# Key and query scratch with the rows of a map side by side: key loads with 64 outer rows in place of four

## The chip, the cores and the metric

One core of one Trainium2 chip runs the whole program. The metric is the device time of one execution in microseconds (us). TensorE (PE), VectorE (DVE), ScalarE (ACT), GpSimd (POOL) and SyncE (SP) each take their instructions in order; transfers run on 16 DMA engines and are issued by SP or ACT.

## The reference

One inference step of a backbone of two layers. 1024 latent tokens and 128 context tokens go through the same weights. Each layer has three groups of heads: differential attention (four heads of 64, two softmax maps per head), a bidirectional gated DeltaNet and a bidirectional mLSTM (four heads each, in chunks), then an output projection and a SwiGLU. The attention, cut to what matters here:

```python
def diff_attention(q, k, v, lam):            # q, k: (B, tokens, 4 heads, 2 maps, 64)
    ...
        s = jnp.einsum('bqhmd,bkhmd->bhmqk', qi, k).astype(jnp.float32) * scale
        p = jax.nn.softmax(s, axis=-1)
        w = p[:, :, 0] - lam * p[:, :, 1]
        return jnp.einsum('bhqk,bkhe->bqhe', w.astype(v.dtype), v)
...
    k_all = jnp.concatenate([axial_rope(ak), k_ctx.astype(ak.dtype)], axis=1)
    a_out = diff_attention(axial_rope(aq), k_all, v_all, diff_lambda(lqk, lam_init))
```

Latent queries attend to 1024 latent and 128 cached keys, context queries to the 128 context keys.

## The kernel before

Latent and context tokens stand in one row of NT = 1152 columns, in three groups of 384 (`GW`). A layer is a sequence of stages: the projections and the preparation of the three mixers (`w_in`), the attention beside the scan of the DeltaNet and the mLSTM (`mixers`), the output projection and the feed-forward part. No order is written out by hand: each engine's instructions are put in order by a scheduler at build time, which plans the whole program with costs of its own. It also gives every transfer one of a few completion semaphores, so that an issue can have to wait until an earlier transfer with the same one has landed.

Products are made in pieces of fp32r: a value is split into a high part (an ACT copy) and a rest (a DVE subtraction). Queries and keys go through DRAM scratch in that form. `blk_a` projects a block, applies the rotary embedding to its two parts p (the even and the odd elements of a head's 64), and `put` splits each of them into `kh` (two buffers of 128 rows, high and rest) and stores it: `put_k` into KD with one transfer, 128 outer rows on both sides, `put_q` into QD with two, one for high and one for rest, whose DRAM side has four outer rows (one for each pair of head and map). Both are issued by SP.

In the attention stage a head loads two tiles K, one per map m, and V, then goes through its queries in blocks of 256 (the last has the 128 context queries). A K tile has 128 partitions: 32 rows of p = 0 and 32 of p = 1 in the high part, then the same of the rest, each row 1280 keys long. It is one transfer whose DRAM side, `(l p)`, has four outer rows of 32 inner ones. A Q tile holds the high queries in both halves of the partitions, so that a product with K adds both parts of the key, and the rest of the queries beside it; each half is one transfer with 64 outer rows and, inside, m and l. All of these loads are issued by ACT, between its own copies and exponentials. There are three buffers for K, so that the first map's K of the next head can be loaded early, while the second has to wait until the head before has used its first.

```python
for hl in range(2):
    nc.tensor.matmul(p[:, :w], lhsT=q[:, m, hl, 128 * j:128 * j + 128],
                     rhs=K[m][:, 128 * ks[0]:128 * ks[0] + w], start=hl == 0, stop=hl == 1)
nc.vector.tensor_scalar(out=e[:, GW * i:GW * i + w], in0=p[:, :w], scalar1=0.125, ..., accum_out=mx[:, i:i + 1])
```

These are the scores s (L1250) and the DVE pass over them (L1251); ACT's exponential follows (L1256), the difference of the maps, the transposes t and the output o.

Beside the attention run the last inverses of the DeltaNet's chunks (`prep2`: matmuls into px, L879 to L909, each waiting for small copies, T and X on ACT, qs and qq on DVE) and then the scan (matmuls into z and y), whose operands SP loads from scratch (rd, rm, vr, v, qk, cq; L1062 loads qk).

Of the kernel before, what the change touches and what calls it, by code (L numbers as in the profile page):

```python
# [9 lines left out]
F32 = mybir.dt.float32  # L10
# [7 lines left out]
P = 128  # L18
# [4 lines left out]
NT = NL + NC  # L23
# [47 lines left out]
class Kern:  # L71
# [362 lines left out]
    def open_s(self, l):  # L434

        S = self.S = {}
        dt = lambda n, shape: self.dr.tile(shape, F32, name=f"{n}{l}")
        S["BT"] = dt("BT", [P, 6, CVO])
        S["CQK"] = dt("CQK", [P, 4, NT])
        S["V1"] = dt("V1", [NCH, P, H, 65])  # L440
        S["BC"] = dt("BC", [NCH, P, 512])
        S["QD"] = dt("QD", [8, 2, 64, NT])
        S["KD"] = dt("KD", [2, 2, 2, P, NT + P])
        S["VD"] = dt("VD", [10, P, 512])
        S["ND"] = dt("ND", [2, NCH, P, H, P])
        S["RD"] = dt("RD", [2, NCH, P, 1024])
        S["GR"] = dt("GR", [2, 16, NT])
        S["VK"] = dt("VK", [NCH, P, 768])
        S["RM"] = dt("RM", [2, NCH, P, 768])
        S["CAT"] = dt("CAT", [KB, P, NT])  # L450
        ed, pe = ExitStack(), ExitStack()
        self.dn = ed.enter_context(self.pool("psdn", PSUM))
        self.pp = pe.enter_context(self.pool("pspp", PSUM))
        return ed, pe
# [472 lines left out]
    def put(self, dst, src, w):  # L927

        t = self.t(self.pr, [P, 2, GW], "kh", 2, F32R)[:, :, :w]
        self.nc.scalar.copy(t[:, 0], src)  # L930
        self.nc.vector.tensor_sub(t[:, 1], src, t[:, 0].bitcast(F32))
        if len(dst) == 1:
            self.nc.sync.dma_start(dst[0], t.bitcast(F32))
        else:
            for i in range(2):
                self.nc.sync.dma_start(dst[i], t[:, i].bitcast(F32))

    def put_k(self, hf, p, cols, src, w):
        self.put([self.S["KD"][hf, :, p, :, cols].rearrange("l r t -> r l t")], src, w)

    def put_q(self, hf, p, cols, src, w):
        self.put([self.S["QD"][4 * hf:4 * hf + 4, hl, 32 * p:32 * p + 32, cols] for hl in range(2)], src, w)

    def blk_a(self, l, qk, hf, u):

# [265 lines left out]
    def attention(self, l):  # L1211

        nc, S, at, pa = self.nc, self.S, self.at, self.pa
# [9 lines left out]
        for h in range(H):  # L1223
            K = []
            for m in range(2):
                k = self.t(at, [P, NT + P], "K", 3, F32R)
                r = 64 * (h % 2) + 32 * m
                nc.scalar.dma_start(k.bitcast(F32), S["KD"][h // 2].rearrange("l p r t -> (l p) r t")[:, r:r + 32, :])
                K.append(k)
            V = self.t(at, [P, 10, 128], "V", 2)  # L1230
            nc.scalar.dma_start(V, S["VD"][:, :, 128 * h:128 * h + 128].rearrange("s p e -> p s e"))
            for q0 in range(0, NT, 256):
                nq = min(256, NT - q0)
                q = self.t(at, [P, 2, 2, 256], "Q", 3, F32R)
                for hh in range(2):
                    nc.scalar.dma_start(q[64 * hh:64 * hh + 64, :, :, :nq].bitcast(F32), S["QD"][2 * h:2 * h + 2, :, :, q0:q0 + nq].rearrange("m l p t -> p m l t"))
                ctx = q0 >= NL
                kt = [9] if ctx else list(range(9))
                groups = [kt] if ctx else [kt[0:3], kt[3:6], kt[6:9]]
# [1 line left out]
                for j in range(nq // 128):  # L1241
                    es, zs = [], []
                    for m in range(2):
                        e = self.t(at, [P, NT], "e", 4)
                        mx = self.t(at, [P, 4], "mx", 4)
                        for i, ks in enumerate(groups):
                            w = 128 * len(ks)
                            p = self.ps(pa, "s", 2)
# [24 lines left out]
                    for i, ks in enumerate(groups):  # L1273
                        n = len(ks)
                        p = self.ps(pa, "t", 1)
# [278 lines left out]
```

## Time and profile before

| What | before |
|---|---|
| median of 3 runs | 3789.91 us (3785.78 to 3790.86) |
| profiled execution, its time | 3786.69 us |
| its span | 3784.9 us |
| PE busy | 3537.8 us (93%) |
| DVE busy | 2294.3 us (61%) |
| ACT busy | 1135.1 us (30%) |
| POOL busy | 655.4 us (17%) |
| DMA moved | 434.12 MB, mean 115 GB/s |

The span is the time from the first to the last instruction of the profiled execution. Busy times leave out the issue of transfers. PEclk is the clock that was granted to PE, as a share of the full one. "q" behind an engine's name is its queue, where transfers are issued; in a chain of waits a transfer's piece is the time for which the chain rested on it.

### The profile page before, as it was taken

What the parts mean: (1) busy time and instruction counts of PE and PEld (TensorE: products, weight loads), DVE (VectorE), ACT (ScalarE), POOL (GpSimd) and SP (SyncE); (2) the same over time, 40 slices, a digit from 0 to 9 for tenths busy, and PEclk for the clock granted to TensorE, in tenths of its full rate; (3) what the DMA queues carried; (4) which work ended last, traced back from release to release, by engine and by line L of the source; (5) the groups of instructions that cost most, each with busy time, mean ns of one, the idle gap of its engine ahead of it and who ended that gap; (6) DMA issues with size and microseconds to landing.
All of it is one profiled execution on the core that took longest, in us unless ns stands there. A gap on an engine that the chain in (4) does not pass through costs nothing.

```text
span 3784.9 us, 59404 instructions
## 1 busy us (share of the span) xinstructions
PE 3537.8 (93%) x22770; PEld 3372.2 (89%) x22770; DVE 2294.3 (61%) x5361; ACT 1135.1 (30%) x2383; POOL 655.4 (17%) x903
## 2 busy tenths in 40 slices
PE   7999979988999999999999998889889999999998
PEld 6997777887899999999989877778778999999997
DVE  7896677778455566654475568377775434333435
ACT  5323316445241111111243431244553311111111
POOL 2014231455020000000020234025631000000001
PEclk8999988999899999999999999889899999999999
DMA  5376624864212222221132663467442111111111
GB/s 208 134 249 232 221 80 122 235 201 144 84 59 84 78 84 83 91 78 48 59 110 96 220 230 102 130 162 227 132 142 67 34 39 46 46 38 40 51 45 56
DMA packets 277090, 434.12 MB, mean 115 GB/s; under 512 B 24648, under 2 KB 186504, under 8 KB 276552
## 3 DMA queue, kind: packets, MB, share of 16 engines
q1 hardware_dynamic: 213336, 289.68, 23.7%
q10 hardware_dynamic: 63472, 140.66, 12.3%
q8 instruction: 180, 2.95, 0.3%
q14 instruction: 102, 0.84, 0.1%
HBM read 315.85 MB, written 114.39 MB: 114 GB/s over the span
## 4 chain that ended last, share of the span: by engine, by line
PE 75%; DMA 10%; DVE 9%; issue 3%; ACT 1%; POOL 1%; SPq 0%; ACTq 0%; POOLq 0%; DVEq 0%
PE pd L189 6%; PE pd L190 6%; PE pd L191 6%; PE pg L191 5%; PE pu L190 5%; PE pu L191 5%; PE pu L189 5%; PE pg L190 5%; PE pg L189 5%; PE dn L189 4%; PE dn L190 4%; PE dn L191 4%; DMA K<-KD 3%; PE s L1250 3%; PE o L1284 2%
## 5 line engine op out<-in xcount | busy, mean ns | idle before, releaser
L362 DVE SCALAR_TENSOR_TENSOR x<-pd,mod,x 128x256 f32<-128x256 f32 (+1 forms) x832 | 405.0, 514 | 598.6 <-PE pd L191 597.4
L183 ACT CAST wh<-wr 128x1024 fp32r<-128x1024 f32 (+1 forms) x219 | 229.1, 1047 | 873.8 <-PE pu L190 462.1
L184 DVE TENSOR_TENSOR wl<-wr,wh 128x1024 fp32r<-128x1024 f32 (+1 forms) x219 | 268.7, 1233 | 167.6 <-ACT wh L183 167.1
L189 PE MATMUL pd<-hh,wh 128*128 128x384 f32 x1056 | 359.3, 340 | 7.3 <-DVE x L362 5.1
L189 PE MATMUL pg<-uh,wh 128*128 128x384 f32 x1056 | 357.2, 338 | 2.6 <-ACT uh L342 2.6
L190 PE MATMUL pg<-ul,wh 128*128 128x384 f32 x1056 | 357.9, 339 | 1.2 <-DVE ul L347 1.2
L299 POOL TENSOR_TENSOR nacc<-nacc,nsq 128x384 f32<-128x384 f32 x48 | 52.2, 1087 | 1770.7 <-issue 1572.5
L189 PE MATMUL pu<-uh,wh 128*128 128x384 f32 x1056 | 355.8, 337 | 0.0
L190 PE MATMUL pu<-ul,wh 128*128 128x384 f32 x1056 | 355.8, 337 | 0.0
L190 PE MATMUL pd<-hl,wh 128*128 128x384 f32 x1056 | 355.5, 337 | 0.0
L191 PE MATMUL pg<-uh,wl 128*128 128x384 f32 x1056 | 354.7, 339 | 0.0
L191 PE MATMUL pd<-hh,wl 128*128 128x384 f32 x1056 | 354.2, 337 | 0.0
L191 PE MATMUL pu<-uh,wl 128*128 128x384 f32 x1056 | 350.7, 337 | 0.0
L189 PE MATMUL dn<-uh,wh 128*128 128x384 f32 x864 | 299.4, 347 | 5.7 <-ACT gw L956 4.4
L190 PE MATMUL dn<-ul,wh 128*128 128x384 f32 x864 | 298.3, 345 | 0.0
L191 PE MATMUL dn<-uh,wl 128*128 128x384 f32 x864 | 297.8, 345 | 0.1
L1250 PE MATMUL s<-K,Q 128*128 128x384 f32 (+1 forms) x800 | 222.9, 389 | 61.2 <-DMA K<-KD 23.5
L1251 DVE TENSOR_SCALAR_CACHE_REDUCE e<-s 128x384 f32<-128x384 f32 (+1 forms) x400 | 208.8, 540 | 76.4 <-PE s L1250 72.3
L189 PEld LDWEIGHTS pd<-hh,wh 128*128 128x128 f32 x1056 | 198.7, 188 | 18.6 <-issue 7.7
L189 PE MATMUL dn<-wh,uh 128*128 128x256 f32 (+1 forms) x624 | 184.6, 296 | 24.1 <-DVE gw L558 19.7
L1250 PEld LDWEIGHTS s<-K,Q 128*128 128x128 f32 x800 | 136.4, 205 | 78.4 <-DVE e L1251 33.5
L189 PEld LDWEIGHTS pg<-uh,wh 128*128 128x128 f32 x1056 | 199.5, 189 | 4.5 <-ACT uh L342 2.8
(354 smaller groups left out, 8224.4 us busy)
## 6 DMA issues: line engine op xcount, KB each, us to landing
wr<-in_w_gu_dram ACTq DMA_DIRECT2D x88, 512.0 KB
aw<-in_w_mod_dram SPq DMA_DIRECT2D x96, 256.0 KB
wr<-in_w_dn_dram ACTq DMA_DIRECT2D x44, 512.0 KB
wr<-in_w_st_dram ACTq DMA_DIRECT2D x36, 512.0 KB
rd<-RD SPq DMA_DIRECT2D x36, 512.0 KB
aw<-in_w_mod_dram SPq DMA_DIRECT2D x32, 512.0 KB
Q<-QD ACTq DMA_DIRECT2D x64, 256.0 KB
RM<-em SPq DMA_DIRECT2D x36, 384.0 KB
```

The costliest lines, as they stand in the source:

```text
L183: nc.scalar.copy(hi, r)
L184: (eng or nc.vector).tensor_tensor(out=lo, in0=r, in1=hi.bitcast(F32), op=ALU.subtract)
L189: mm(out, lhsT=wh, rhs=xh, start=start, stop=False)
L190: mm(out, lhsT=wh, rhs=xl, start=False, stop=False)
L191: mm(out, lhsT=wl, rhs=xh, start=False, stop=stop)
L299: (nc.gpsimd if k in PST else nc.vector).tensor_tensor(out=self.acc[g], in0=self.acc[g], in1=s, op=ALU.add)
L362: nc.vector.scalar_tensor_tensor(out=x[g][k][:, lo:hi], in0=ps[:, lo:hi], scalar=gate[:, k, cnd:cnd + 1], in1=x[g][k][:, lo:hi], op0=ALU.m ...
L1250: nc.tensor.matmul(p[:, :w], lhsT=q[:, m, hl, 128 * j:128 * j + 128], rhs=K[m][:, 128 * ks[0]:128 * ks[0] + w], start=hl == 0, stop=hl == 1)
L1251: nc.vector.tensor_scalar(out=e[:, GW * i:GW * i + w], in0=p[:, :w], scalar1=0.125, scalar2=None, op0=ALU.mult, op1=ALU.max, accum_out=mx[ ...
L1284: nc.tensor.matmul(po, lhsT=WT[i][:, a], rhs=V[:, kx, :], start=kx == kt[0], stop=kx == kt[-1])
```

## The change

Both scratches get another order of their axes, in which the row r of a map and its part p are neighbours: a map's 64 rows, (r p), lie side by side. The K load then has 64 outer rows per transfer, one transfer for the high half of the partitions and one for the rest; the Q load has one transfer for each half and each of high and rest, four in place of two; `put` stores queries as it stores keys, with one transfer of 128 outer rows. The number of bytes is the same everywhere.

```diff
--- before.py
+++ after.py
@@ -439,8 +439,8 @@
         S["CQK"] = dt("CQK", [P, 4, NT])
         S["V1"] = dt("V1", [NCH, P, H, 65])
         S["BC"] = dt("BC", [NCH, P, 512])
-        S["QD"] = dt("QD", [8, 2, 64, NT])
-        S["KD"] = dt("KD", [2, 2, 2, P, NT + P])
+        S["QD"] = dt("QD", [2, 2, P, 2, NT])
+        S["KD"] = dt("KD", [2, 2, P, 2, NT + P])
         S["VD"] = dt("VD", [10, P, 512])
         S["ND"] = dt("ND", [2, NCH, P, H, P])
         S["RD"] = dt("RD", [2, NCH, P, 1024])
@@ -929,17 +929,13 @@
         t = self.t(self.pr, [P, 2, GW], "kh", 2, F32R)[:, :, :w]
         self.nc.scalar.copy(t[:, 0], src)
         self.nc.vector.tensor_sub(t[:, 1], src, t[:, 0].bitcast(F32))
-        if len(dst) == 1:
-            self.nc.sync.dma_start(dst[0], t.bitcast(F32))
-        else:
-            for i in range(2):
-                self.nc.sync.dma_start(dst[i], t[:, i].bitcast(F32))
+        self.nc.sync.dma_start(dst.rearrange("l r t -> r l t"), t.bitcast(F32))
 
     def put_k(self, hf, p, cols, src, w):
-        self.put([self.S["KD"][hf, :, p, :, cols].rearrange("l r t -> r l t")], src, w)
+        self.put(self.S["KD"][hf, :, :, p, cols], src, w)
 
     def put_q(self, hf, p, cols, src, w):
-        self.put([self.S["QD"][4 * hf:4 * hf + 4, hl, 32 * p:32 * p + 32, cols] for hl in range(2)], src, w)
+        self.put(self.S["QD"][hf, :, :, p, cols], src, w)
 
     def blk_a(self, l, qk, hf, u):
 
@@ -1225,15 +1221,19 @@
             for m in range(2):
                 k = self.t(at, [P, NT + P], "K", 3, F32R)
                 r = 64 * (h % 2) + 32 * m
-                nc.scalar.dma_start(k.bitcast(F32), S["KD"][h // 2].rearrange("l p r t -> (l p) r t")[:, r:r + 32, :])
+                for lk in range(2):
+                    nc.scalar.dma_start(k[64 * lk:64 * lk + 64].bitcast(F32), S["KD"][h // 2, lk, r:r + 32].rearrange("r p t -> (r p) t"))
                 K.append(k)
             V = self.t(at, [P, 10, 128], "V", 2)
             nc.scalar.dma_start(V, S["VD"][:, :, 128 * h:128 * h + 128].rearrange("s p e -> p s e"))
+            r0 = 64 * (h % 2)
             for q0 in range(0, NT, 256):
                 nq = min(256, NT - q0)
                 q = self.t(at, [P, 2, 2, 256], "Q", 3, F32R)
                 for hh in range(2):
-                    nc.scalar.dma_start(q[64 * hh:64 * hh + 64, :, :, :nq].bitcast(F32), S["QD"][2 * h:2 * h + 2, :, :, q0:q0 + nq].rearrange("m l p t -> p m l t"))
+                    for hl in range(2):
+                        nc.scalar.dma_start(q[64 * hh:64 * hh + 64, :, hl, :nq].bitcast(F32),
+                                     S["QD"][h // 2, hl, r0:r0 + 64, :, q0:q0 + nq].rearrange("(m r) p t -> (r p) m t", m=2))
                 ctx = q0 >= NL
                 kt = [9] if ctx else list(range(9))
                 groups = [kt] if ctx else [kt[0:3], kt[3:6], kt[6:9]]
```

In the changed kernel the K load stands at L1225, the Q load at L1235, V at L1228 and `put` at L932.

**ACT's queue at the start of attention in layer 0, before:** the loads of the first head (KD_122, QD_121 and VD_123 are the scratches) between copies of T and X for the inverses.

```order
L1228 DMA K_7842<-KD_122 128x1x1280
L861 COPY X_676_3285<-Nd_2455 32x4x32 x4
L1228 DMA K_7844<-KD_122 128x1x1280
L1231 DMA V_7846<-VD_123 128x10x128
L1236 DMA Q_7848<-QD_121 64x4x256 x2
L864 COPY T_680_3289<-cv_3297 32x4x32 x2
L864 COPY T_681_3290<-cv_3363 32x4x32 x2
L1236 DMA Q_8016<-QD_121 64x4x256 x2
L1236 DMA Q_8184<-QD_121 64x4x256
```

The same place in the changed kernel:

```order
L1225 DMA K_7830<-KD_122 64x1280
L861 COPY X_676_3285<-Nd_2455 32x4x32 x4
L1225 DMA K_7830<-KD_122 64x1280
L1225 DMA K_7833<-KD_122 64x1280 x2
L864 COPY T_680_3289<-cv_3297 32x4x32 x2
L1228 DMA V_7836<-VD_123 128x10x128
L861 COPY X_678_3287<-Nd_2456 32x4x32 x4
L864 COPY T_681_3290<-cv_3363 32x4x32 x2
L1235 DMA Q_7838<-QD_121 64x2x256 x4
L1235 DMA Q_8008<-QD_121 64x2x256
L864 COPY T_680_3289<-cv_3297 32x4x32 x2
```

The two K loads are four, Q's loads for a block are four, and both copies of T that stood behind Q's first block now stand ahead of it.

**PE at the same place, before:** the last px matmuls ahead of the first scores.

```order
L893 MATMUL px_3783<-Nd_2455,qs_744_3774 32x32 x4
L893 MATMUL px_3789<-Nd_2456,qs_746_3781 32x32 x4
L901 MATMUL px_3795<-T_680_3289,w_733_3715 64x64 x4
L901 MATMUL px_3802<-T_681_3290,w_734_3723 64x64 x4
L1250 MATMUL s_7854<-K_7842,Q_7848 128x384 x2
L1250 MATMUL s_7858<-K_7842,Q_7848 128x384 x2
L909 MATMUL px_3809<-X_676_3285,qq_3800 64x64 x4
```

In the changed kernel, from the same px matmul (px_3795) on:

```order
L901 MATMUL px_3795<-T_680_3289,w_733_3715 64x64 x4
L901 MATMUL px_3802<-T_681_3290,w_734_3723 64x64 x4
L909 MATMUL px_3809<-X_676_3285,qq_3800 64x64 x4
L909 MATMUL px_3816<-X_678_3287,qq_3807 64x64 x4
L879 MATMUL px_3839<-cv_3297,w_755_3823 32x32 x4
L879 MATMUL px_3846<-cv_3363,w_756_3831 32x32 x4
L887 MATMUL px_3853<-qs_758_3844,Nd_2455 32x32 x4
L887 MATMUL px_3859<-qs_760_3851,Nd_2456 32x32 x4
L893 MATMUL px_3865<-Nd_2455,qs_758_3844 32x32 x4
L1250 MATMUL s_7846<-K_7830,Q_7838 128x384
L1250 MATMUL s_7850<-K_7830,Q_7838 128x384
L1250 MATMUL s_7846<-K_7830,Q_7838 128x384
```

Seven more rows of px, 28 matmuls, now stand ahead of the first scores.

**SP in the preparation of layer 0, where the queries are stored, before** (kh is the split block, CQK, GR and VK are scratches of the mLSTM, rope the rotary table):

```order
L936 DMA QD_121<-kh_4793 4x32x384 x2
L936 DMA QD_121<-kh_4798 4x32x384 x2
L961 DMA rope_4933<-in_rope_dram 128x2x256
L936 DMA QD_121<-kh_4869 4x32x384
L936 DMA QD_121<-kh_4874 4x32x384
L756 DMA c_487_2464<-CQK_118 128x4x128
L790 DMA gr_2495<-GR_126 2x8x128
L790 DMA gr_2524<-GR_126 2x8x128
L936 DMA QD_121<-kh_4869 4x32x384
L936 DMA QD_121<-kh_4874 4x32x384
```

In the changed kernel:

```order
L932 DMA QD_121<-kh_4793 128x2x384
L932 DMA QD_121<-kh_4797 128x2x384
L957 DMA rope_4929<-in_rope_dram 128x2x256
L756 DMA c_487_2464<-CQK_118 128x4x128
L790 DMA gr_2495<-GR_126 2x8x128
L790 DMA gr_2524<-GR_126 2x8x128
L932 DMA QD_121<-kh_4867 128x2x384
L932 DMA QD_121<-kh_4871 128x2x384
L768 DMA VK_127<-vk_2471 128x768
```

Two transfers for a kh have become one, and the mLSTM's loads stand ahead of the second pair.

## Rows read from the trace of the kernel before

**Rows 1.** The chain that ended last, shares of the span by line.

```profile
PE pd L189 6%; PE pd L190 6%; PE pd L191 6%; PE pg L191 5%; PE pu L190 5%; PE pu L191 5%; PE pu L189 5%; PE pg L190 5%; PE pg L189 5%; PE dn L189 4%; PE dn L190 4%; PE dn L191 4%; DMA K<-KD 3%; PE s L1250 3%; PE o L1284 2%
```

**Rows 2.** Engines in the attention stages: stretch, length, busy time of each, PEclk, DMA, GB/s.

```profile
545.00:945.00 400.00, 340.50 (x3013) 310.81 (x3011) 306.75 (x1023) 200.20 (x486) 165.76 (x211) 0.90 0.61 175
...
2415.00:2815.00 400.00, 338.52 (x2709) 311.38 (x2708) 293.04 (x980) 188.92 (x447) 166.43 (x207) 0.88 0.61 175
```

**Rows 3.** The chain that ended last, in order of time: start, length, what.

```profile
549.15 24.47 DMA Q<-QD
574.59 1.62 PE s L1250 x4
...
2421.59 14.11 DMA K<-KD
2435.71 16.06 DMA Q<-QD
2451.91 1.62 PE s L1250 x4
...
2739.64 12.88 DMA K<-KD
```

**Rows 4.** Engines in eleven load stretches of the attention stages, and their sum.

```profile
549.00:574.00 25.00, 10.37 (x163) 9.32 (x160) 6.89 (x22) 2.20 (x8) 0.00 (x0) 0.53 0.65 157
653.00:667.20 14.20, 10.93 (x137) 9.62 (x133) 10.72 (x39) 6.86 (x19) 2.63 (x3) 0.98 0.65 157
...
2421.50:2452.00 30.50, 15.59 (x262) 13.90 (x255) 10.80 (x34) 3.14 (x11) 0.00 (x0) 0.55 0.66 167
...
sum 183.10, PE 117.74 PEld 108.05 DVE 111.16 ACT 60.83 POOL 64.23; mean PE 10.70 PEld 9.82 DVE 10.11 ACT 5.53 POOL 5.84
```

**Rows 5.** Engines in five stretches of these stages without such a load, sum.

```profile
sum 296.00, PE 281.82 PEld 267.29 DVE 247.69 ACT 154.14 POOL 151.72; mean PE 56.36 PEld 53.46 DVE 49.54 ACT 30.83 POOL 30.34
```

**Rows 6.** Engines in two short stretches: Q alone moves, K alone moves.

```profile
635.50:637.50 2.00, 2.00 (x17) 1.93 (x17) 1.91 (x9) 1.31 (x2) 0.00 (x0) 1.00 0.92 230
671.00:675.00 4.00, 4.00 (x38) 3.18 (x37) 2.31 (x11) 1.14 (x5) 0.55 (x1) 0.70 0.24 99
```

**Rows 7.** DMA issues: queue, count, size of one.

```profile
Q<-QD ACTq DMA_DIRECT2D x64, 256.0 KB
...
K<-KD ACTq DMA_DIRECT2D x16, 640.0 KB
```

**Rows 8.** Timeline of ACT and its queue at both starts; [idle before <-releaser].

```profile
546.31 1.12 ACTq L1228 DMA_DIRECT2D K<-KD  x1
...
549.15 16.90 ACTq L1236 DMA_DIRECT2D Q<-QD  x2
566.15 0.30 ACT L864 COPY T<-cv 32x128 f32<-32x128 f32 x1 [17.45 <-issue]
...
2450.56 0.62 ACT L864 COPY T<-cv 32x128 f32<-32x128 f32 x2 [24.14 <-DMA Q<-QD]
```

**Rows 9.** Waits of SP's queue: total us, times, longest.

```profile
SPq L1062 <- DMA K<-KD: 20.4, 2, 10.2
```

**Rows 10.** The chain again: a write of KD and the longest of QD.

```profile
277.70 4.75 DMA KD<-kh
...
302.04 10.61 DMA QD<-kh
```

**Rows 11.** Engines while the chain rested on a QD write.

```profile
299.00:316.00 17.00, 11.52 (x40) 8.25 (x40) 9.60 (x21) 4.18 (x9) 3.47 (x5) 0.67 0.57 184
```

**Rows 12.** Issues by line: count, duration in ns min/median/max, first and last start.

```profile
L1228 ACTq DMA_DIRECT2D K<-KD x16: 537/558/1124, 546.3 to 2739.6; - x16
...
L1236 ACTq DMA_DIRECT2D Q<-QD x80: 581/590/16234, 549.1 to 2776.8; - x80
...
L182 ACTq DMA_DIRECT2D wr<-in_w_gu_dram x88: 334/334/335, 1006.3 to 3681.4; - x88
...
L1149 SPq DMA_DIRECT2D cq<-CQK x32: 359/371/662, 692.7 to 2697.8; - x32
```


## Prediction

> **What bounds the kernel now.** I read the chain of work that ended last first, then cut its one suspicious item into stretches. TensorE (PE) carries three quarters of the chain, but one transfer, the load of K from the scratch KD, holds 3% of it [rows 1], that is 0.03 × 3784.9 = 113 us, the largest share of any transfer. All of it lies in the two attention stages, one per layer, each 400 us long, in which PE is busy 340.50 and 338.52 us and DVE 306.75 and 293.04 [rows 2]: 60 us of PE are idle in each. In order of time the reader should see the chain come to rest on a load at every head: at a stage's start on the first Q (24.47 us in layer 0; K 14.11 and then Q 16.06 in layer 1) with the first score matmul right behind, and later on K again, the shortest time 12.88 us [rows 3]. There are seven K pieces, four Q pieces and one V piece of that kind.
>
> I then asked for engine time in eleven stretches, one for each load that the chain rests on in these stages (in two places two neighbouring ones together). They last 183.1 us and PE works 117.74 of them: 65.4 us idle, more than half of the 121 us idle in both stages. The two starts alone leave 25.0 − 10.37 = 14.6 and 30.5 − 15.59 = 14.9 idle; the stretch at 653 us leaves only 3.3 of 14.2 [rows 4], since px work (the inverses of the DeltaNet chunks) stands in PE's order ahead of the waiting scores. In five stretches of the same stages without such a load and near full clock PE works 281.82 of 296 us, 95.2% [rows 5]. So the loads are what is left to win, and PE's cover is what limits the win.
>
> Why the loads are slow shows in a stretch in which K moves alone: a DMA share of 0.24, that is four of 16 engines, and 99 GB/s. Where Q moves alone, from 64 outer rows, the share is 0.92 and the rate 230 GB/s [rows 6]. K is 640 KB a map, Q 256 KB a half [rows 7]. A Q queued behind K ends only when its share on the four busy engines ends.
>
> The slow K does harm beyond PE. ACT issues these loads in order with its copies: one pair of Q issues held its queue for 16.90 us, and the copy of T behind it, which px waits for, started after 17.45 us of idling; in layer 1 a copy of T waited 24.14 us for Q [rows 8]. SP, which feeds the scan, lost 20.4 us at one of its loads to K [rows 9].
>
> **The change, part by part.** The sum is made against the profiled execution, 3786.69 us (span 3784.9); the median of the three runs is 3.2 us above it.
>
> *A, the starts of the two stages.* From the first K issue to the first score: 574.59 − 546.31 = 28.3 us [rows 3, 8] and 2451.91 − 2421.59 = 30.3 us [rows 3]. In the new order the same bytes stand ahead of the first score: K twice and V, 3 × 655,360 B (V has K's size: 10 × 128 rows of 128 floats), and Q, 2 × 262,144 B [rows 7]: 2.49 MB. At the 230 GB/s of the 64-row Q loads that takes 10.8 us; the first issue (1.12 us in layer 0, rows 8), the last landing and SP's transfers for px, which run beside it on the same engines, come on top, and I take 14.5. The waits shrink by 13.8 and 15.8. The new PE order has 28 more px matmuls ahead of the first score, and the T copies that they need now stand ahead of Q in ACT's order, so px fills the shorter wait and is not itself held up; I charge 2.6 for it. **A = −27**, bounds −15 (half is eaten by px, which runs from copy to copy) and −40 (px hides all of it and the clock comes back sooner: the 10.37 + 15.59 us of PE work in these stretches ran at a granted clock of 0.53 and 0.55, near the lower of its two levels, 1.2 GHz [rows 4]; at 2.4 it would be some 13 us less).
>
> The Trainium skill speaks against loading in halves: "DMA: Bandwidth & Descriptors" (Rules for kernel authors) says that transfers to two partition halves serialize and one of 128 partitions should be used, and "SBUF — State Buffer" (Door 1: The DMA port swizzle) gives 196 GB/s for 64 partitions against 328 for 128 at 1 MiB. The Q row, with loads of both halves in flight, shows 230, between the two. By 196 the 10.8 us would be 12.7, by 328 they would be 7.6: the halves may leave some 3 us a start unused, and do not turn the sign.
>
> *B, the later loads.* The nine other stretches hold 183.1 − 55.5 = 127.6 us with 117.74 − 25.96 = 91.8 us of PE work [rows 4]: 35.8 idle. K alone falls from 12.88 us or more to 655,360 B / 230 GB/s = 2.8 plus some 2 for issue and landing. That saving, 8 or more, exceeds the idle of most stretches, and the Q, V and SP loads behind K are freed too. At the clean share [rows 5] 91.8 us of work take 96.4: −31.2 at best. Behind a vanished wait comes the next one, DVE's pass over the scores or ACT's exponential, so I take two thirds: **B = −22**, bounds −8 (a shorter wait only hands over to the next) and −31.2.
>
> *C, the writes of QD.* 48 writes with 4 outer rows become 24 with 128. The chain rests on QD writes four times, the longest 10.61 us; a KD write, which has 128 outer rows already, stands there with 4.75 [rows 10]. What waits is ACT's next conversion (two kh buffers), and behind it work of the mLSTM that PE needs. But PE is mostly covered: around the longest it worked 11.52 of 17 us [rows 11]. KD's own writes keep shape and number. **C = −6**, bounds 0 and −15.
>
> *D, more issues on ACT.* 16 K issues at a median 558 ns become 32 with one outer dimension, as wr has (334): +1.8 us. 80 Q issues at 590 ns become 160 with two, as cq has (371 on SP): +12.2 [rows 12]. ACT is busy 200.20 and 188.92 of 400 us [rows 2], and its cover is its idling before exponentials; if that were gone, all 14.0 would count. **D = +3**, bounds 0 and +14. On SP 24 issues fall away, off the path: 0.
>
> Sum: −27 − 22 − 6 + 3 = −52. 3786.7 − 52 = 3734.7 for a profiled run; 3789.9 − 52 = **3738 us** for the median. At the bounds: −15 − 8 + 14 = −9 and −40 − 31.2 − 15 = −86.
>
> **The rivals.**
> *The waits change hands* (0.18). The new order of all engines differs throughout, since the scheduler planned it afresh; PE and DVE stand near each other in the stages [rows 2], so a shorter load wait may be taken over by DVE, or by ACT between them. For it: the stretch at 653 us, where PE idles 3.3 of 14.2 [rows 4]. Against it: the starts, where ACT works 2.20 of 25 us and PE 10.37 [rows 4]. Time: A and B at their low bounds, C nothing, D +5: −18, 3772 us.
>
> *The whole chain gives* (0.13). Every load wait goes, the clock stays up, SP's loads arrive early: A and B at their high bounds, C −15, and D nothing: −86, 3704 us. For it: copies of T and SP's loads stood behind K [rows 8, 9]. Against it: PE cannot be busier than all the time, and most stretches have little idle.
>
> *ACT's queue becomes the bound* (0.06), the slower case. Each Q and K issue may have to wait for the landing of an earlier transfer that shares its semaphore, and ACT's copies and exponentials wait behind it, as once in layer 0 for 17.45 us [rows 8]. With twice as many issues back to back at each of the six later head changes such a stop can recur there. It decides from 52 / 6 = 8.7 us a change on; at 12 us it costs 72 and the time is 3790 + 20 = 3810 us. Against it: what has to land does so in about a third of the time.
>
> *The change doesn't spread the loads* (0.03). If 64 outer rows stayed on four engines, only D would be left, +3 to +14: about 3797 us. The Q row, 64 outer rows at a share of 0.92, speaks against it [rows 6]. The Trainium skill ("DMA: Bandwidth & Descriptors", Why a DMA increments its semaphore by 16 and not by 1) says that the engines are the largest number up to 16 that divides the outer counts of both sides: 4 for 4 and 128, 16 for 64 and 64; the trace agrees on both.
>
> **How the numbers follow.** My own case has 0.60, with a range of its own from 3718 to 3758 (terms A and B each off by a third). The range that leaves out no more than 0.2 reaches into both neighbours: 3700 to 3775. 0.2% is 7.6 us, about what a measurement of this kernel can tell from no change. Faster by more: 0.60, 0.13 and nearly all of the 0.18, together 0.90. Within it: 0.04, from the edges of the second and the last case. Slower: 0.06.
>
> **What would show it.** In the profile after: K loads at a DMA share near 0.9, not 0.24; first score 14 to 16 us after the first K issue in both layers; PE busy over 90% of both stages, which end some 20 us sooner each; no copy of T with 17 us of idling ahead of it; K gone from the head of the transfers in the chain; QD pieces under 6 us; Q issues near 370 ns. I would be wrong if stretches at the head changes stay as long with DVE or ACT named as releaser, if ACT stops on semaphores at its Q issues, or if the fresh order moves px or the scan so that the stages end on something else.

## The result, and the profile after

Four runs of the changed kernel have a median of 3697.69 us (3694.80 to 3699.32), beside 3790.39 for the kernel before (four runs): ratio 0.9756, 95% interval 0.9739 to 0.9773. It is faster by 92.7 us, 40 us under the forecast of 3738 and 2 us under the range.

The page after, its head and engines, one row of the costliest groups and one of the DMA issues:

```profile
span 3697.5 us, 59430 instructions
...
PE 3521.8 (95%) x22770; PEld 3355.3 (91%) x22770; DVE 2290.0 (62%) x5361; ACT 1136.6 (31%) x2383; POOL 665.5 (18%) x903
...
L1250 PE MATMUL s<-K,Q 128*128 128x384 f32 (+1 forms) x800 | 226.5, 388 | 32.1 <-DVE e L1251 23.1
...
Q<-QD ACTq DMA_DIRECT2D x128, 128.0 KB
```

The row of the scores before:

```profile
L1250 PE MATMUL s<-K,Q 128*128 128x384 f32 (+1 forms) x800 | 222.9, 389 | 61.2 <-DMA K<-KD 23.5
```

PE's idle time ahead of the scores has halved, and what ends most of it is now DVE's pass over them, no longer the load of K. The chain of work that ended last reaches back only to 2700 us in this profile, so it cannot be laid beside [rows 1, 3 and 10]. I cut both spans at four kinds of mark instead, all of them start times of TensorE's rows: a layer's last dn matmul (end of the preparation), its first score, then the first dn of layer 1 or the first pg of layer 1's feed-forward (end of attention and of what follows it). The column "rest" is from the first score to that mark; in layer 0 it holds the whole feed-forward too. Times in us, layer 0 and layer 1:

| kernel (profiled run) | preparation | start | rest | last part | span |
|---|---|---|---|---|---|
| before | 546.1, 506.4 | 28.5, 30.1 | 1340.8, 474.7 | 858.3 | 3784.9 |
| after | 526.5, 486.8 | 18.1, 18.7 | 1338.3, 449.8 | 859.3 | 3697.5 |
| e1 queries only | 524.8, 486.4 | 26.9, 26.4 | 1370.5, 491.0 | 859.7 | 3785.7 |
| e2 keys only | 552.0, 508.1 | 18.2, 19.0 | 1324.8, 455.9 | 858.4 | 3736.5 |
| e3 two wide writes | 527.5, 485.8 | 16.9, 17.1 | 1335.5, 463.3 | 857.9 | 3703.9 |
| e4 narrow writes | 545.7, 506.1 | 16.9, 17.1 | 1341.3, 463.2 | 858.8 | 3749.2 |
| e6 whole key load | 526.9, 486.5 | 14.7, 15.0 | 1331.6, 443.1 | 859.2 | 3677.1 |
| e7 two query loads | 525.3, 485.1 | 17.3, 19.0 | 1329.8, 453.8 | 858.4 | 3688.8 |
| e8 both of these | 525.7, 485.4 | 13.8, 13.5 | 1335.5, 455.8 | 858.9 | 3688.7 |
| e9 two query loads, old keys | 526.5, 485.5 | 28.5, 30.3 | 1364.5, 478.0 | 859.0 | 3772.4 |
| e10 spare narrow writes | 553.8, 508.1 | 17.6, 20.2 | 1330.3, 447.4 | 858.9 | 3736.4 |
| e11 spare wide writes | 528.2, 486.8 | 19.2, 16.6 | 1343.4, 458.3 | 858.8 | 3711.2 |
| e12 spare narrow, ACT's queue | 554.3, 516.4 | 20.7, 17.7 | 1336.9, 446.2 | 859.8 | 3751.9 |

The first two rows hold the answer: of 87.4 us, the two preparations give 39.2 (19.6 each), the two starts 21.8, the rest 27.4 (2.5 and 24.9), and the last part takes 1.0 back. The attention stages together, 49 us, are near what was forecast; the preparation, forecast at 6, is where the surplus lies.

What happened in it shows in the engine times of the preparation, from an early point with nearly the same number of matmuls behind it to its end, layer 0 and layer 1. Columns: stretch, length, busy time of PE, PEld, DVE, ACT and POOL with their instructions, PEclk, DMA share, GB/s. Before:

```profile
250.00:546.10 296.10, 271.55 (x1762) 239.35 (x1761) 218.32 (x431) 85.28 (x232) 100.10 (x167) 0.95 0.56 185
...
2150.00:2421.80 271.80, 246.10 (x1938) 220.77 (x1936) 175.07 (x378) 76.67 (x214) 79.72 (x135) 0.95 0.49 158
```

After:

```profile
250.00:526.50 276.50, 262.94 (x1767) 233.38 (x1765) 218.28 (x433) 84.83 (x232) 102.19 (x167) 0.98 0.59 198
...
2116.00:2369.70 253.70, 239.65 (x1939) 215.51 (x1938) 175.37 (x379) 77.09 (x217) 83.99 (x136) 0.98 0.51 169
```

The number of matmuls is the same within five. PE's idle time in layer 0 falls from 296.10 − 271.55 = 24.6 us to 13.6. And the same matmuls take 8.6 us less, because the granted clock rises from 0.95 to 0.98: if PE stands at one of its two levels, 1.2 or 2.4 GHz, a mean of 0.95 means a tenth of the stretch at the lower one, 0.98 a twenty-fifth. So less idle time is paid twice here, once itself and once in the clock. In layer 1 it is 25.7 to 14.1 idle and 6.5 us of work.

Who waits is told by the waits in these stretches (us in total, times, longest). Before, layer 0:

```profile
DVE em L775 <- DMA RM<-em: 16.0, 9, 4.3
...
ACT kh L930 <- DMA QD<-kh: 7.2, 4, 2.7
...
ACT gw L956 <- DMA QD<-kh: 6.1, 1, 6.1
PE pp L793 <- DVE em L775: 4.5, 3, 2.7
...
PE pp L771 <- DMA c<-CQK: 2.5, 1, 2.5
```

After, layer 0:

```profile
DVE em L775 <- DMA RM<-em: 9.0, 5, 2.4
```

ACT's waits for QD, 13.3 us, are gone, as forecast. But waits for transfers that the diff does not touch have shrunk or gone as well: for RM, which SP writes from em, and for CQK, which it reads. Behind the first stood DVE's next em, and behind that PE's pp (products of the DeltaNet's and the mLSTM's chunks). PE's own waits at pp, 7.0 us before, do not occur in the view after.

The attention, after: first K issue to first score, and first to last score, of each layer:

```profile
526.70:544.60 17.90, 15.94 (x274) 14.38 (x273) 11.30 (x35) 4.49 (x16) 0.00 (x0) 0.63 0.96 252
544.60:894.80 350.20, 323.69 (x2676) 293.57 (x2677) 283.37 (x967) 186.75 (x450) 165.78 (x207) 0.93 0.58 168
2369.10:2388.40 19.30, 14.57 (x266) 13.13 (x265) 10.80 (x34) 4.32 (x15) 0.00 (x0) 0.64 0.95 231
2388.40:2741.00 352.60, 325.51 (x2445) 297.74 (x2446) 290.36 (x958) 188.45 (x432) 167.59 (x208) 0.93 0.64 184
...
528.00:531.70 3.70, 3.39 (x77) 3.22 (x78) 2.65 (x10) 0.55 (x2) 0.00 (x0) 0.93 0.96 244
```

PE works 92% of both stages from first to last score, and in the last row, in which K's first two halves move, the DMA share is 0.96 at 244 GB/s (SP's transfers included) where K alone showed 0.24 and 99 [rows 6].

### The profile page after: what moved, and what is told of

Same layout as the page of the kernel before. It is cut to its first block, busy times and chain, and to the rows that moved or that the text cites. A ratio compares the mean times of both kernels' runs of the same rounds, so it can differ in the third digit from the quotient of the medians.

```text
span 3697.5 us, 59430 instructions
## 1 busy us (share of the span) xinstructions
PE 3521.8 (95%) x22770; PEld 3355.3 (91%) x22770; DVE 2290.0 (62%) x5361; ACT 1136.6 (31%) x2383; POOL 665.5 (18%) x903
## 5 line engine op out<-in xcount | busy, mean ns | idle before, releaser
L191 PEld LDWEIGHTS pg<-uh,wl 128*128 128x128 f32 x1056 | 199.1, 189 | 3.7
L190 PEld LDWEIGHTS pg<-ul,wh 128*128 128x128 f32 x1056 | 199.2, 189 | 3.3 <-DVE ul L347 2.2
```

What stands on the lines that cost most here:

```text
L190: mm(out, lhsT=wh, rhs=xl, start=False, stop=False)
L191: mm(out, lhsT=wl, rhs=xh, start=False, stop=stop)
```

## The experiments

Each stands beside the kernel before, timed with it (3790.7 us for e1 to e4, 3790.1 for e7 and e9 to e11, 3791.4 for e6 and e8, 3789.5 for e12). Diffs are against the kernel after, cut to the lines that show the edit. W is the theory that wide QD writes carry the preparation's 39 us, K the rival that the faster K loads carry the gain.

**e1, queries only.** KD, its writes and its loads as before; QD as after. K's rows and Q's rows then stand in different orders, so that scores pair other elements; e2 does the same the other way round.

```diff
-        S["KD"] = dt("KD", [2, 2, P, 2, NT + P])
+        S["KD"] = dt("KD", [2, 2, 2, P, NT + P])
-                for lk in range(2):
-                    nc.scalar.dma_start(k[64 * lk:64 * lk + 64].bitcast(F32), S["KD"][h // 2, lk, r:r + 32].rearrange("r p t -> (r p) t"))
+                nc.scalar.dma_start(k.bitcast(F32), S["KD"][h // 2].rearrange("l p r t -> (l p) r t")[:, r:r + 32, :])
```

> Queries in the new order (one wide write a split block, four loads a block), keys in the old one (K loaded from four outer rows). Theory W (the writes of QD from 128 outer rows freed the preparation, some 38 us over two layers; the K loads the attention, some 50): the preparation keeps its gain, both starts and the head changes lose theirs: 3740 to 3755 us. Rival K (nearly all came from the K loads, and the preparation only moved with a lucky order): 3775 to 3795 us. Rival Q (the loads of Q, not of K, held the attention): 3700 to 3715 us.

3788.22 us, ratio 0.9996 (0.9987 to 1.0006). The time is the rival's, but not for its reason: both preparations are as short as after (524.8 and 486.4), and the attention gives it all back; the rest is 46 us longer than before. In its waits of ACT between first and last score of layer 0:

```profile
ACT e L1255 <- DMA Q<-QD: 12.5, 1, 12.5
ACT m L1204 <- DMA Q<-QD: 11.2, 1, 11.2
```

ACT stops at Q loads behind the slow K, with four Q loads a block in place of two. This is the mechanism of the slower rival, "ACT's queue becomes the bound", with some 12 us a stop as it was priced; the kernel after, with the same Q loads and the fast K, waits for Q at most 3.6 us at a time there. How much of the 46 us these stops cost is not shown.

**e2, keys only.** QD, its writes and its loads as before; KD as after.

```diff
-        S["QD"] = dt("QD", [2, 2, P, 2, NT])
+        S["QD"] = dt("QD", [8, 2, 64, NT])
```

> Keys in the new order, queries as before (two writes with four outer rows a split block, two loads a block). The order of all engines up to the attention of layer 0 is that of the kernel before. Theory W: the attention gains its 50 us, the preparation nothing: 3730 to 3745 us, with dn of layer 0 ending near 546 us as before. Rival K: 3698 to 3715 us. By the term D of the prediction, fewer issues on ACT than after should show as 3 us at most.

3734.66 us, ratio 0.9855 (0.9839 to 0.9871), as theory W has it. The preparations are no shorter than before (552.0 and 508.1), the starts are those of after, and start and rest together give 56 us. This kernel is nearly the forecast one: everything in the attention, nothing in the preparation, and a time 3 us from the forecast. That it is so near is in part luck: its preparations are 7.6 us longer than before, and start and rest give 10 us more than the 46 that A, B and D came to.

**e3, two wide writes.** The layout after, but each half of a split block written by itself: 48 QD writes of 128 outer rows.

```diff
-        self.put(self.S["QD"][hf, :, :, p, cols], src, w)
+        self.put([self.S["QD"][hf, hl, :, p, cols] for hl in range(2)], src, w)
```

> The changed kernel, but each split block of queries is stored by two transfers (high, rest), each with 128 outer rows. Theory W (the width of the writes matters): 3695 to 3706 us. Rival N (the number of transfers and of issues on SP matters): 3715 to 3735 us.

3706.04 us, ratio 0.9781 (0.9765 to 0.9797); preparations 527.5 and 485.8. The number of writes costs nothing there.

**e4, narrow writes.** The loads of after, but QD padded between groups of 32 rows, so that a write has four outer rows again: 48 writes.

```diff
-        S["QD"] = dt("QD", [2, 2, P, 2, NT])
+        S["QD"] = dt("QD", [2, 2, 4, 65 * NT])
```

> The changed kernel, but the maps in QD are set apart by one unused row, so that the stores of queries have four outer rows again, two transfers a split block; all loads are those of the changed kernel. The order up to the attention of layer 0 is that of the kernel before. Theory W: the preparation loses what it gained, 3730 to 3742 us, with dn of layer 0 ending near 546 us and half-clock stretches in the preparation as before. Rival (loads did it all): 3698 to 3706 us.

3744.50 us, ratio 0.9875 (0.9859 to 0.9890), 2 us above what W gave. Starts as in e3 to a tenth, rest within 6 us, and the preparations back at 545.7 and 506.1. With the outer rows of a write, 4 or 128, the preparations change by 38.5 us and the attention hardly. The planner's order changes with them, though: up to the attention of layer 0, e4 has the order of the kernel before and e3 one of its own.

**e10, e11, e12, spare writes.** e4 doesn't say whether ACT's wait for its two kh buffers cost the time, as the forecast had it, or the delay of other transfers. So the changed kernel gets spare writes whose data nobody uses, right behind each QD write, from a constant tile into scratch that is never read; XD is padded in e10, unpadded in e11.

```diff
-        self.put(self.S["QD"][hf, :, :, p, cols], src, w)
+        q = self.put(self.S["QD"][hf, :, :, p, cols], src, w)
+        with self.tc.issue_after(q.ins):
+            for i in range(2):
+                self.nc.sync.dma_start(self.S["XD"][hf, p, i, :, :32, cols], self.con[:, :w])
```

> The changed kernel with two more writes right behind each of the 24 QD writes: 4 outer rows, 192 KB, from a constant tile into scratch that nobody reads. No engine waits for them; they only use SP's queue and four DMA engines, in the number and size of the old QD writes. Theory 'engines': the preparation's 39 us came from narrow writes that hold four DMA engines, so that SP's other transfers (RM above all, for which DVE waited 16 us in layer 0) land late. Then layer 0's preparation ends at 540 to 546 us, as with narrow QD writes, and the time is 3725 to 3745. Rival 'buffer': what cost was ACT's wait for the kh buffers that the narrow QD writes read. They are left free here, so the preparation ends at 525 to 530 us and the time is 3694 to 3706.

> The control to the spare narrow writes: the same extra writes of the same bytes, with 128 outer rows in place of 4. Theory 'engines': 9.4 MB more over 16 engines are hardly felt, 3694 to 3708 us, the preparation of layer 0 ends at 525 to 531. Rival: the bytes or the 48 issues on SP cost by themselves; then this kernel is as late as the narrow one, over 3715.

> The spare narrow writes again, 48 of 4 outer rows beside the changed kernel's own QD writes, but issued on ACT's queue, right behind ACT's conversions, in place of SP's. Theory 'engines': four busy DMA engines slow whoever uses them, whatever the queue; the preparation of layer 0 ends at 540 us or later as with SP's spare narrow writes (553.8), the time is 3722 to 3745. Rival 'queue': what hurts is that SP's later transfers stand behind the narrow ones in SP's own queue; on ACT's queue the preparation ends at 525 to 532, the time is 3697 to 3715, with 48 more issues on ACT of some 0.5 us.

e10: 3741.01 us, ratio 0.9871 (0.9858 to 0.9885). The preparations are 27 and 21 us longer than after; 553.8 is even past the expected 546, perhaps since the kernel's own writes come on top. Its waits in layer 0, and one of SP's queue:

```profile
DVE em L776 <- DMA RM<-em: 15.5, 6, 6.4
ACT kh L931 <- DMA KD<-kh: 11.2, 4, 6.2
ACT kh L931 <- DMA QD<-kh: 6.7, 2, 5.8
PE pp L772 <- DMA c<-CQK: 5.7, 2, 3.0
PE pp L794 <- DVE vk L768: 4.1, 1, 4.1
PE pp L794 <- DVE em L776: 2.2, 2, 1.8
...
SPq L942 <- DMA XD<-con: 4.3, 3, 1.5
```

The wait for RM is back at its old size, KD and QD, both of 128 outer rows, are late as well, and PE waits 12.0 us at pp. The spare writes are not without waiters after all: SP's queue stops 14.7 us in all for XD, at issues of other transfers. Engines in the preparation of layer 0:

```profile
250.00:553.80 303.80, 276.09 (x1740) 242.88 (x1738) 214.29 (x427) 83.58 (x229) 100.59 (x167) 0.92 0.58 194
```

e11, the same bytes in 128 outer rows: 3714.58 us, ratio 0.9803 (0.9789 to 0.9816), with preparations of 528.2 and 486.8:

```profile
250.00:528.20 278.20, 260.39 (x1725) 231.14 (x1724) 214.47 (x427) 83.14 (x228) 102.90 (x167) 0.99 0.62 212
```

Its DVE waits 14.0 us for RM too, nearly as long as in e10, but PE has 17.8 us of idle time in place of 27.7, none of it at pp, and a clock of 0.99. So DVE's wait for RM does not measure the loss; PE's waits at pp do better. The whole time is above its 3694 to 3708 by the rest, 13.5 us longer than after, where no load has changed.

e12, the spare narrow writes on ACT's queue: 3759.99 us, ratio 0.9925 (0.9909 to 0.9942), preparations 554.3 and 516.4. The time is above both expectations, the preparation of layer 0 where "engines" put it. The narrow writes no longer stand in SP's own queue, and DVE waits for RM longer still; ACT now has stops of its own:

```profile
DVE em L776 <- DMA RM<-em: 25.0, 8, 5.6
ACT kh L931 <- DMA QD<-kh: 16.4, 5, 9.8
ACT e L798 <- DMA XD<-con: 9.1, 1, 9.1
...
SPq L933 <- DMA XD<-con: 8.2, 4, 2.6
```

So the loss does not need narrow writes in SP's own queue: they delay the transfers beside them from ACT's as well, though here some of it may be ACT's own stops. The traces show two ways in which they do. Other transfers land later: from issue to the last update of its semaphore, a wide QD write of 384 KB takes 4.6 us in the mean after and 4.4 in e11, but 7.1 in e10 and 8.2 in e12 (preparation of layer 0). And later issues stop for the narrow write itself, with which they can share a semaphore: SP's queue waits 8.3 us for QD before, 14.7 for XD in e10 and 36.3 in e12, but 0.2 after and in e11. Which of the two weighs more is open. Nor are the kh buffers excluded, as this experiment meant to do: ACT's waits for KD and QD writes out of kh are 17.9 us in e10 and 21.6 in e12, against 6.3 after and 8.2 in e11, as those writes land late too.

**e9, two query loads, old keys.** e1 with QD in yet another order (head, half, map), so that a block has two Q loads as before; it too pairs other elements.

```diff
-        S["QD"] = dt("QD", [2, 2, P, 2, NT])
+        S["QD"] = dt("QD", [2, 2, 2, 2, 64, NT])
-        S["KD"] = dt("KD", [2, 2, P, 2, NT + P])
+        S["KD"] = dt("KD", [2, 2, 2, P, NT + P])
```

> Old KD with its slow loads of 4 outer rows; QD in yet another order (head, half, map), so that a block has two Q loads of 64 outer rows and 256 KB as in the kernel before, and two QD writes of 64 outer rows for each split block. As in e1 the rows of K and Q pair differently, so other scores are computed. Theory 'queue': in e1 the preparation gained 41 us and the attention lost as much because four Q loads a block stand on ACT's queue behind the slow K (ACT stopped 12.5 and 11.2 us at two of them). With two a block the loss goes: 3740 to 3758. Rival: the loss came from the planner's other order of the attention, or from Q on 16 engines meeting K on four, not from the number of loads: 3775 to 3795.

3774.24 us, ratio 0.9956 (0.9944 to 0.9969): between both, nearer the rival. It is 14 us faster than e1, less than a fresh order alone may move (see below), so the number of Q loads is not shown to be the cause. The preparation is short again (526.5, 485.5), and the rest is still 27 us longer than before, with loads of the same number and size.

**e7, two query loads.** The kernel after with that QD: 80 Q loads of 256 KB in place of 160.

> The changed kernel with half the Q loads: QD ordered by head, half and map, two loads of 256 KB a block, 80 in place of 160 issues on ACT, for 48 QD writes of 64 outer rows in place of 24 of 128. The forecast's term D (3 us, bounds 0 and 14) by itself: if ACT's idling covers the issues, 3690 to 3700; if each issue counts in full, 3680 to 3688. If the writes' number or their 64 rows cost something, above 3700.

3690.65 us, ratio 0.9741 (0.9727 to 0.9755). The issues by line (count, duration in ns min/median/max), after:

```profile
L1225 ACTq DMA_DIRECT2D K<-KD x32: 452/500/747, 526.7 to 2657.3; - x32
...
L1235 ACTq DMA_DIRECT2D Q<-QD x160: 581/590/3738, 533.4 to 2693.1; - x160
```

and e7:

```profile
L1238 ACTq DMA_DIRECT2D Q<-QD x80: 581/607/1821, 533.7 to 2691.1; - x80
```

That is 160 × 0.590 − 80 × 0.607 = 45.8 us less of issuing on ACT for 7 us of time: the cover that the forecast counted on is there.

**e6, whole key load, and e8.** KD's rows in the order (row, component, half), so that a map is one load of 128 outer rows, with Q loaded to every second partition. e8 is e6 with e7's Q loads.

```diff
-                for lk in range(2):
-                    nc.scalar.dma_start(k[64 * lk:64 * lk + 64].bitcast(F32), S["KD"][h // 2, lk, r:r + 32].rearrange("r p t -> (r p) t"))
+                nc.scalar.dma_start(k.bitcast(F32), S["KD"][h // 2, r:r + 32].rearrange("r p l t -> (r p l) t"))
-                        nc.scalar.dma_start(q[64 * hh:64 * hh + 64, :, hl, :nq].bitcast(F32),
+                        nc.scalar.dma_start(q[hh:128:2, :, hl, :nq].bitcast(F32),
```

> The changed kernel with K in one load of 128 outer rows in place of two of 64 (KD's rows ordered by row, component, half; Q loaded to every second partition, so that the pairs stay right). 16 K issues in place of 32. Theory 'halves' (the Trainium skill, 'DMA: Bandwidth & Descriptors': two half-partition transfers serialize): about 3 us a start and some at the six head changes, 3680 to 3692. Rival: at 0.92 of the engines the two halves already use what there is, 3694 to 3702; Q's strided partitions could cost above that.

> Both at once: K in one load of 128 outer rows, and Q in two loads a block (QD by head, half, map). 96 fewer issues on ACT than in the changed kernel. If the two edits add up, the two-load kernel's 3691 less what the whole K load gives, 3675 to 3690; if neither is worth more than the planner's reordering, 3688 to 3702.

e6: 3679.85 us, ratio 0.9705 (0.9692 to 0.9718), the fastest here and 18 us under the kernel after. The starts fall to 14.7 and 15.0. While the first two K loads of layer 0 move:

```profile
527.80:532.60 4.80, 4.38 (x95) 4.07 (x95) 3.21 (x11) 1.13 (x4) 0.00 (x0) 0.82 0.92 288
```

288 GB/s at a share of 0.92, where the halves had 244 at 0.96 (SP's transfers are in both). The rule of the Trainium skill that the forecast weighed, "DMA: Bandwidth & Descriptors" (Rules for kernel authors), is to use one transfer over 128 partitions in place of two to its halves. The trace agrees in direction, and the starts are 3.4 and 3.7 us shorter than after, where some 3 had been estimated. But the planner also put V and Q earlier: in ACT's timeline V is issued at 528.14 and the first Q at 528.62, against 532.16 and 533.38 after. How much of the 3.4 and 3.7 us is due to which was not separated. e8: 3689.95 us, ratio 0.9731 (0.9718 to 0.9745), with the shortest starts (13.8, 13.5) and a rest 16.5 us longer than e6's. The edits don't add up.

The rest is the weak place of all these comparisons. After, e3, e4, e10, e11 and e12 have the same attention loads, and their rests sum to 1777.7 to 1804.5 us, 27 us apart. The planner orders each program afresh, which is the likely reason; each row is also one execution, and those scatter (before, e2 and e4 have the same order up to the attention of layer 0, and its preparation ends at 546.1, 552.0 and 545.7). e7's 7 us and what e6 gains beyond its starts lie within this spread; the preparations (1010 to 1015 with wide writes alone, 1052 to 1071 with narrow ones) and e6's starts lie outside it.

The order is a rival in the preparation too, since no run changes the width of the writes and keeps the order. Against it speaks that the width sorts all of them: up to the attention of layer 0, the eight kernels with wide writes alone have four different orders on SP and end at 524.8 to 528.2 us, the five with narrow ones have three and end at 545.7 to 554.3.

## Why the prediction was wrong

**C, the writes of QD: the step that failed.** It gave −6, bounds 0 and −15; measured are −39.2 in the preparations. The forecast charged the one stretch in which the chain rested longest on a QD write, found PE at work for 11.52 of 17 us there [rows 11], and took the waiting party to be ACT's conversion. In its place the runs show that the 24 narrow writes of a layer delayed transfers beside them all over the stage, CQK, RM and KD among them, and that these waits stood under other names. e10 and e12 show it: spare narrow writes whose data nobody uses lengthen the first preparation by 27 and 28 us. e11 excludes their bytes, e3 their number. The upper bound lacked the clock as well: 36% and 44% of the saving (6.5 of 18.1 us in layer 1's stretch, 8.6 of 19.6 in layer 0's) is PE doing the same work faster. Two signs were to be had from the profile before. The row of the 17 us itself has a granted clock of 0.67 [rows 11]. And the chain rested on QD writes in three more places:

```profile
291.23 7.15 DMA QD<-kh
...
386.20 10.42 DMA QD<-kh
...
2264.37 8.70 DMA QD<-kh
```

With the 10.61 us of [rows 10] these are 36.9 us, more than twice the upper bound of C. The work of PE beside such a piece is no cover for it, since the chain is what ended last. The sum is no forecast of the gain either: a wide write can rest in the chain too, as KD's 4.75 us shows.

**A, the starts: right in kind, some 20% off.** −21.8 (10.4 and 11.4) for −27. From the first K issue the first score comes after 17.9 and 19.3 us, not 14.5. The bytes move as fast as assumed, 252 GB/s at a share of 0.96 in layer 0, but the first Q is issued 6.7 us behind the first K there (before, 2.8 [rows 8]), with copies of T and X between. e6, with whole K loads and an earlier Q, has 14.6 and 15.8; which of the two it owes them to is open.

**B, the later loads: right within what can be told.** With D it was −19; the rest gives −27.4 here and, over the six kernels with the same loads, −11 to −38, on average −23. That layer 0 gives 2.5 and layer 1 24.9 is probably the order of the moment: in e10 it is 10.5 and 27.3, in e4 nothing and 11.5.

**D, more issues on ACT: the price wrong, the cover right.** 32 K issues at 500 ns and 160 Q issues at 590 make 110.4 us against 56.1 [rows 12], 54 more, not 14: I had given the new loads the durations of loads in other places, and a Q issue cost no less for having fewer dimensions. e7 takes 46 of them away for 7 us at most.

**The rivals.** "The whole chain gives" named the time that came nearest, 3704, by another sum: its A and B did not reach their bounds, and C went past its own. "ACT's queue becomes the bound" did not happen here; no copy of T stands behind 17 us of idling (8.59 is the longest at the first start, and px ends it). e1 shows such stops with the slow K. "The waits change hands" came true in name, DVE's pass now ends most of the waits ahead of the scores, 11.6 us in layer 0 where it was 9.4, but it did not eat the gain.

**Open.** With the old K, e1 and e9 have a rest 46 and 27 us longer than before, which takes back what the preparation gives. ACT's stops at Q are seen in e1, and e9's part may be the planner's order alone; no run separates them. Nor was it tried which of the delayed transfers carries how much of the preparation, or whether they are late because the narrow writes slow them, because their issue waits for a shared semaphore, or because ACT waits for kh.

## What to carry to other kernels

Look at the outer rows of every write, not only of those that the chain rests on: here the narrow ones were paid by their neighbours, under their names. Where PE is nearly full, its idle time can cost twice, once more in the granted clock. With a planner that orders everything afresh, compare stage by stage, and distrust a gain of 10 us in a stage whose own work has not changed. A spare transfer whose data nobody uses tests what a transfer does to others, but look at the issuing queues too: they may still wait for it.

## What the runs showed of the hardware

- 48 writes of 4 outer rows and 192 KB, whose data nobody uses, lengthen the two preparations by 49 us from SP's queue (e10) and by 57 from ACT's (e12); in 128 outer rows (e11) by 2.
- A write of 192 KB with 4 outer rows lands 7.9 us after its issue in the mean (QD before, preparation of layer 0), one of the same size with 128 outer rows after 3.6 (e3).
- The granted clock of the same preparation, about 1,750 matmuls, is 0.99 with 17.8 us of PE idle time (e11), 0.98 with 13.6 (after), 0.95 with 24.6 (before), 0.94 with 32.8 (e12: 304.30 − 271.51) and 0.92 with 27.7 (e10): lower where more is idle, but not in step.
- A load of 64 outer rows takes ACT's queue 500 ns (K) and 590 ns (Q) to issue; the whole K load of 128 took 390 at the median, 326 at the shortest.
